# A norm's sum of squares in a two-layer transformer: one accumulator for both streams, and the last square added on VectorE

## Chip, cores and metric

The kernel runs on one core of a Trainium2 chip. The metric is the device time of one execution in microseconds (us), as a median over runs. Smaller is better. Engines are named as in the profile: PE is TensorE (matrix products), PEld its weight loads, DVE VectorE, ACT ScalarE, POOL GpSimd and SP SyncE, which here only issues transfers.

## What is computed

Two streams of 256 tokens with 1024 features each, the latent stream `x` and a context `ctx`, go through two blocks. Block 0 has a gated feed-forward network, a short convolution mixer and a second feed-forward network. Block 1 has a feed-forward network, grouped-query attention and a last feed-forward network; the context is dropped after the attention has read it. Ahead of each of the six parts both streams (in the last part only the latent one) are normalised:

```
def _rms(t, g):
    t32 = t.astype(jnp.float32)
    y = t32 * lax.rsqrt(jnp.mean(t32 * t32, axis=-1, keepdims=True) + NORM_EPS)
    return y.astype(t.dtype) * g

def _modulate(t, g, shift, scale):
    return _rms(t, g) * (1 + scale) + shift

lat = lat + 0.5 * mod[:, 0, 2] * _swiglu(_modulate(lat, norm_g[i, 0], mod[:, 0, 0], mod[:, 0, 1]), ...)
```

The change concerns `mean(t32 * t32)`, the sum of 1024 squares for each token. Everything else stays.

## The kernel before

**Layout.** Both streams lie side by side in one SBUF tile `x` of 128 partitions by 8 feature tiles by 512 tokens: `x[:, k, :]` holds features 128k to 128k+127, columns 0 to 255 are the latent stream (stream 0), columns 256 to 511 the context (stream 1). Features lie on partitions, so a sum over features is a sum over the eight tiles k, done element by element, and then a sum over 128 partitions, done on PE.

**The sum of squares.** `square_add(k, c0, c1)` (lines 254 to 268) is called once for each feature tile when that tile of `x` is final. ACT squares the tile into a buffer `sq` (line 258; one of three buffers that share the tag `gm` with other temporaries). For k = 0, DVE copies the square into the stream's accumulator `acc` (line 264); for k = 1 to 6 DVE adds it to `acc` (line 266), one instruction of 128x256 for each stream. The last square, k = 7, is not added: `accs[s, "last"]` remembers where it lies.

`rms_sum(s, parts)` (lines 270 to 285) then makes, for each of the stream's two tiles of 128 tokens, one product with a column of ones for `acc` and one for the last square, accumulated in PSUM (line 275). In float32 each such product is two records of PE. ACT takes the square root (line 280) and DVE the reciprocal (line 284). `rms_all` (line 290) spreads the 256 reciprocals over all partitions with two more products (line 293). Then `scaled` and `norm_k` or `Blocks.block` (lines 302 to 404) make the normalised tiles: a DVE instruction at line 305, ACT instructions at lines 315, 397 or 402, and DVE instructions at 316 or 398.

**Where it is called.** There are six places, and eleven streams in all:

- The first norm (lines 898 and 1055). The eight squares follow the arrival of `x`, both streams at once, while PE runs 39 products of ones on ones (`fill(WARM)`, line 1054), which stand ahead of the sums in PE's order. The order of PE, DVE, ACT and SP in this part is written out by hand (`FIRST_STEPS`).
- Four tails of `project` with `tail_norm` (line 517): after the first feed-forward network (ahead of the convolution), after the convolution, after the second feed-forward network, and after the third (ahead of attention). Here feature tiles 0 to 5 are finished for both streams at once. Tiles 6 and 7 are finished last (lines 634 to 643), first for stream 0, then for stream 1, so that stream 0's norm can start while PE still makes stream 1's products.
- One tail with `tail_early` (line 488), after attention, stream 0 only.

**What sets the order.** Outside the hand-ordered parts a planner orders each engine's instructions when the program is built: it goes through the program with a cost model and gives an engine the earliest instruction of the program that is ready. Pending pieces of a norm are put into the program by `flush` in the middle of later products. In the networks at line 784 an edge (line 792) keeps the second weight tile's products behind the last product of `rms_all` on PE. DVE, ACT and PE each work through their queue in the order so fixed. DVE's other work in these places is splitting weights into two halves (line 109, 128x1024) and a reduction of modulation weights (line 178).

Of the kernel before, what the change touches and what calls it, by code (L numbers as in the profile page):

```python
# [9 lines left out]
F32 = mybir.dt.float32  # L10
F32R = mybir.dt.float32r
BF16 = mybir.dt.bfloat16
AF = mybir.ActivationFunctionType
ALU = mybir.AluOpType
AX = mybir.AxisListType

P = 128
D = 1024
KT = D // P
S = 256  # L20
T2 = 2 * S
# [26 lines left out]
def hybrid_kernel(ctx: ExitStack, tc: tile.TileContext, a: dict, out: bass.AP):  # L48
    nc = tc.nc
# [5 lines left out]
    tp = ctx.enter_context(tc.tile_pool(name="tp", bufs=2))  # L55
# [6 lines left out]
    def nm(s):  # L62
        uid[0] += 1
        return f"{s}{uid[0]}"
# [4 lines left out]
    def psmall(s="pq"):  # L69
        return pss.tile([P, T2], F32, tag="sm", name=nm(s))  # L70
# [8 lines left out]
    x = act.tile([P, KT, T2], F32, name="x", tag="x")  # L79
    for q in range(4):  # L80
# [4 lines left out]
    ones = const.tile([P, P], F32, name="ones", tag="ones")  # L85
# [5 lines left out]
        out=const.tile([P, 1], F32, name="silu", tag="silu"), in_=eps_t, func=AF.Silu  # L91
# [132 lines left out]
    def mod_ready(l, ch):  # L224
        while not ((l, ch) in done and done[l, ch] == 8 * streams(l, ch)):
            next_unit()
        return modv[l, ch]

    def scale_of(l, j):

        m = mod_ready(l, 3 * j + 1)
        t = const.tile([P, KT, 2], F32, name=f"A{l}{j}", tag=f"A{l}{j}")
        g = normg[:, l, j, :]
        for v in range(1 if (l, j) == (1, 2) else 2):
            nc.vector.scalar_tensor_tensor(
                out=t[:, :, v], in0=m[:, :, v], scalar=1.0, in1=g, op0=ALU.add, op1=ALU.mult
            )
        return t
# [13 lines left out]
    accs = {}  # L252

    def square_add(k, c0, c1):

        n = c1 - c0
        sq = tp.tile([P, T2], F32, name=nm("sq"), tag="gm", bufs=3)
        nc.scalar.activation(out=sq[:, :n], in_=x[:, k, c0:c1], func=AF.Square)
        for s in range(2):
            if c0 <= s * S < c1:  # L260
                part = sq[:, s * S - c0 : s * S - c0 + S]
                if k == 0:
                    accs[s] = tp.tile([P, S], F32, name=nm("acc"), tag=f"acc{s}", bufs=1)
                    nc.vector.tensor_copy(accs[s], part)
                elif k < KT - 1:
                    nc.vector.tensor_tensor(out=accs[s], in0=accs[s], in1=part, op=ALU.add)
                else:
                    accs[s, "last"] = part

    def rms_sum(s, parts):  # L270

        pq = psmall("ss")
        for i in range(2):
            for n, t in enumerate(parts):
                nc.tensor.matmul(
                    pq[:, S + i : S + i + 1], t[:, i * P : i * P + P], ones[:, 0:1],
                    start=(n == 0), stop=(n == len(parts) - 1),
                )
        rs = tp.tile([P, 2], F32, name=nm("rs"), tag="rs")
        nc.scalar.activation(  # L280
            out=rs, in_=pq[:, S : S + 2], func=AF.Sqrt, scale=1.0 / D, bias=eps_t
        )
        ri = tp.tile([P, 2], F32, name=nm("ri"), tag="ri")
        nc.vector.reciprocal(ri, rs)
        return pq, ri
# [4 lines left out]
    def rms_all(pq, ri):  # L290

        for i in range(2):
            every.append(nc.tensor.matmul(
                pq[:, i * P : i * P + P], ri[:, i : i + 1].to_broadcast([P, P]), ident,
                start=True, stop=True,
            ).ins)
        return pq[:, :S]

    def rms_inv(s, parts):
        return rms_all(*rms_sum(s, parts))  # L300

    def scaled(s, k, A, ri, t=None):
        if t is None:
# [7 lines left out]
    def norm_k(s, k, h, A, B, ri, t=None):  # L311
        hh, hl = pick(h, k, s * S, s * S + S)
        t = scaled(s, k, A, ri, t)
        b = B[:, k, s : s + 1]
        nc.scalar.activation(out=hh, in_=t, func=AF.Identity, bias=b)
        nc.vector.scalar_tensor_tensor(
            out=hl, in0=t, scalar=b, in1=hh.bitcast(F32), op0=ALU.add, op1=ALU.subtract
        )
        return t
# [163 lines left out]
    def flush(n=9):  # L483
        while pending and n:
            pending.pop(0)()
            n -= 1

    def tail_early(l, j, h, z):

        box = {}  # L490

        def tail(m, c0, c1):
            if not box:
                box["A"] = scale_of(l, j)
                box["B"] = mod_ready(l, 3 * j)
                z.shift(box["B"])
            z.put(m, box["A"])
            square_add(m, c0, c1)
            if m < KT - 1:
                return  # L500

            def first():
                box["ri"] = rms_sum(0, (accs[0], accs[0, "last"]))

            def second():
                z.ri = tp.tile([P, S], F32, name=nm("ris"), tag="ris0", bufs=1)
                nc.scalar.copy(z.ri, rms_all(*box["ri"]))

            def rest(part):
                for k in range(4 * part, 4 * part + 4):  # L510
                    norm_k(0, k, h, box["A"], box["B"], z.ri)

            pending.extend((first, second, lambda: rest(0), lambda: rest(1)))

        return tail

    def tail_norm(l, j, h):

        box = {}

        def tail(m, c0, c1):
            square_add(m, c0, c1)
            if m == KT - 1:
                if not box:
                    box["A"] = scale_of(l, j)
                    box["B"] = mod_ready(l, 3 * j)
                s = c0 // S

                def inv():
                    return rms_inv(s, (accs[s], accs[s, "last"]))  # L530

                def rest(part, ri, ks=range(4)):

                    if isinstance(h, Blocks):
                        h.block(s, part, box["A"], box["B"], ri, s == 0, ks)
                    else:
                        for k in ks:
                            norm_k(s, 4 * part + k, h, box["A"], box["B"], ri)

                def both_parts():  # L540
                    ri = inv()
                    for part in range(2):
                        rest(part, ri)

                if s == 0:
                    keep = []

                    def one():
                        keep.append(inv())
                        rest(0, keep[0])  # L550

                    pending.append(one)
                    pending.append(lambda: rest(1, keep[0], range(2)))
                    pending.append(lambda: rest(1, keep[0], range(2, 4)))
                else:
                    flush()
                    pending.append(both_parts)

        return tail
# [19 lines left out]
    def ready():  # L579

        t = const.tile([P, 1], F32, name=nm("ready"), tag="ready")
        nc.scalar.activation(out=t, in_=accs[0][:, :1], func=AF.Sqrt)

    def project(ws, src, nk, gate, tail, tot, late, ev, between=()):

# [307 lines left out]
    def fill(n):  # L893

        for _ in range(n):
            nc.tensor.matmul(idle[:, :P], ones, ones, start=True, stop=True)

    for k in range(KT):
        square_add(k, 0, T2)
# [4 lines left out]
        out=sb1, in0=modb[:, 0, KT : 2 * KT], scalar1=1.0, scalar2=None, op0=ALU.add  # L904
# [147 lines left out]
    queues = [nc.tensor, nc.vector, nc.scalar, nc.sync]  # L1052
    with tc.manual_schedule(engines={e.engine for e in queues}):
        fill(WARM)
        sums = [rms_sum(s, (accs[s], accs[s, "last"])) for s in range(2)]
        for step in FIRST_STEPS.split():
            steps[step[0]](*(int(c) for c in step[1:]))
    done[0, 0] = done[0, 1] = 16
# [22 lines left out]
    for m in range(KT):  # L1081
# [4 lines left out]
        for c0, c1 in ((0, S), (S, T2)) if m == 0 else ((0, T2),):  # L1086
# [18 lines left out]
            out=d2[:, :, 1:], in0=u2[:, :, : S - 1], scalar=convk[:, 0, m : m + 1],  # L1105
            in1=d2[:, :, 1:], op0=ALU.mult, op1=ALU.add,
        )
        nc.vector.scalar_tensor_tensor(
            out=d2[:, :, : S - 1], in0=u2[:, :, 1:], scalar=convk[:, 2, m : m + 1],
            in1=d2[:, :, : S - 1], op0=ALU.mult, op1=ALU.add,  # L1110
# [70 lines left out]
    def q_proj(p):  # L1181
        wq = load_w(a["wq"][p])
        if p == 0:

            ps = [psum("pq")[:, :S] for _ in range(2)]
            order = [(i, k) for k in range(KT) for i in range(2)]
        else:
            ps = psum("pq")
            ps = [ps[:, :S], ps[:, S:], ps]
            order = [(i, k) for i in range(2) for k in range(KT)]  # L1190
        for i, k in order:
            mm3(ps[i], wq(k * 256 + i * P), pick(h, k, 0, S), k == 0, k == KT - 1)
        return ps[2:] or ps
# [60 lines left out]
    pq = [q_proj(0)]  # L1254
# [17 lines left out]
    for kv in range(KVH):  # L1272
# [7 lines left out]
        out=scq, in0=rq[:, :16], scalar1=float(P) ** -0.5, scalar2=None, op0=ALU.mult  # L1280
# [76 lines left out]
    for i in range(2):  # L1357
# [3 lines left out]
        for j in range(4):  # L1361
            c = j % 2 * T2
# [127 lines left out]
```

## Time and profile before

| | |
|---|---|
| median of 3 runs | 1559.67 us (1559.26 to 1561.86) |
| profiled execution, span from its first to its last instruction | 1558.7 us |
| profiled execution, time outside the span | not listed; the median of the runs is 0.97 us over the span |
| busy: PE, PEld, DVE, ACT, POOL | 1549.9, 1422.0, 1281.7, 782.1, 221.6 us |
| PE records of the products at line 275 | 88 |
| DVE copies at line 264, adds at line 266 | 11, 66 |
| granted TensorE clock | 1.000 |

A profile here is one execution. The page lists busy time for each engine. Waits name the engine that waited and the one that released it. The chain of work that ended last is followed backwards from the last instruction and says, at each moment, what the end hung on. A timeline row has start, length, engine, line and the tile written and read; the number behind an x says how many instructions were merged into the row. A windows row gives, for a stretch of time, busy time and instruction counts of PE, PEld, DVE, ACT and POOL, then the granted clock, the share of the DMA engines and GB/s.

### The profile page before, as it was taken

What the parts mean: (1) busy time and instruction counts of PE and PEld (TensorE: products, weight loads), DVE (VectorE), ACT (ScalarE), POOL (GpSimd) and SP (SyncE); (2) the same over time, 40 slices, a digit from 0 to 9 for tenths busy, and PEclk for the clock granted to TensorE, in tenths of its full rate; (3) what the DMA queues carried; (4) which work ended last, traced back from release to release, by engine and by line L of the source; (5) the groups of instructions that cost most, each with busy time, mean ns of one, the idle gap of its engine ahead of it and who ended that gap; (6) DMA issues with size and microseconds to landing.
All of it is one profiled execution on the core that took longest, in us unless ns stands there. A gap on an engine that the chain in (4) does not pass through costs nothing.

```text
span 1558.7 us, 26399 instructions
## 1 busy us (share of the span) xinstructions
PE 1549.9 (99%) x10296; PEld 1422.0 (91%) x10296; DVE 1281.7 (82%) x2030; ACT 782.1 (50%) x1297; POOL 221.6 (14%) x187
## 2 busy tenths in 40 slices
PE   9999999999999999999999999999999999999999
PEld 7898998999888899989999899989999898998888
DVE  5788789799987588968978888968978887888676
ACT  5642553644423366436346466436346455774553
POOL 0012213200000112032042112022042002300000
PEclk9999999999999999999999999999999999999999
DMA  9567467465555425655656635655766843276562
GB/s 371 194 173 200 109 191 193 120 194 161 191 198 178 115 62 136 205 146 130 206 144 158 200 71 136 203 149 130 235 170 170 264 156 114 93 234 219 172 197 74
DMA packets 88253, 263.53 MB, mean 169 GB/s; under 512 B 10816, under 2 KB 12608, under 8 KB 88128
## 3 DMA queue, kind: packets, MB, share of 16 engines
q1 hardware_dynamic: 69408, 230.72, 45.8%
q0 software_dynamic: 16128, 29.37, 11.3%
q10 hardware_dynamic: 2592, 1.76, 0.4%
q8 instruction: 80, 1.31, 0.3%
q14 instruction: 45, 0.37, 0.1%
HBM read 259.45 MB, written 1.05 MB: 167 GB/s over the span
## 4 chain that ended last, share of the span: by engine, by line
PE 96%; DVE 2%; ACT 1%; issue 0%; POOL 0%; DVEq 0%; ACTq 0%; POOLq 0%
PE py L137 9%; PE py L138 9%; PE py L139 9%; PE p L137 7%; PE p L139 7%; PE p L138 7%; PE q L137 5%; PE q L139 5%; PE q L138 5%; PE py L145 2%; PE pu L145 2%; PE pg L145 2%; PE py L147 1%; PE pg L147 1%; PE pu L147 1%; PE pv L138 1%
## 5 line engine op out<-in xcount | busy, mean ns | idle before, releaser
L108 ACT ACTIVATE wh<-wr 128x1024 fp32r<-128x1024 f32 (+2 forms) x446 | 394.5, 912 | 325.2 <-PE py L138 126.1
L109 DVE TENSOR_TENSOR wl<-wr,wh 128x1024 fp32r<-128x1024 f32 (+2 forms) x446 | 456.6, 1048 | 85.9 <-ACT wh L108 66.8
L178 DVE CUSTOM_DVE_ANT_0 junk<-wr,scbc,modb 128x1024 bf16<-128x1024 f32 x213 | 274.7, 1290 | 11.4 <-DMA wr<-in_modT 9.3
L137 PE MATMUL py<-gh,wh 128*128 128x512 f32 (+1 forms) x570 | 213.5, 375 | 0.0
L138 PE MATMUL py<-gl,wh 128*128 128x512 f32 (+1 forms) x570 | 213.3, 374 | 0.0
L139 PE MATMUL py<-gh,wl 128*128 128x512 f32 (+1 forms) x570 | 213.2, 374 | 0.0
L704 POOL TENSOR_SCALAR wr<-wr 128x512 f32<-128x512 f32 x56 | 101.1, 1805 | 541.7 <-DMA wr<-in_w 286.3
L567 DVE SCALAR_TENSOR_TENSOR x<-py,mod,x 128x256 f32<-128x256 f32 x213 | 94.6, 479 | 65.6 <-PE py L139 54.3
L138 PE MATMUL p<-tl,wh 128*128 128x256 f32 x448 | 126.9, 283 | 0.0
L139 PE MATMUL p<-th,wl 128*128 128x256 f32 x448 | 126.9, 283 | 0.0
L137 PE MATMUL p<-th,wh 128*128 128x256 f32 x448 | 126.9, 283 | 0.0
L139 PEld LDWEIGHTS py<-gh,wl 128*128 128x128 f32 x570 | 107.4, 188 | 19.2
L137 PEld LDWEIGHTS py<-gh,wh 128*128 128x128 f32 x570 | 107.5, 189 | 18.3
L138 PEld LDWEIGHTS py<-gl,wh 128*128 128x128 f32 x570 | 107.5, 189 | 17.9
L115 POOL DMA_DIRECT2D w4l<-in_w x56 | 53.8, 960 | 445.7 <-ACT w4l L114 431.9
L137 PE MATMUL q<-bh,wh 128*128 128x256 f32 x320 | 90.8, 284 | 0.8 <-ACT wh L108 0.8
L139 PE MATMUL q<-bh,wl 128*128 128x256 f32 x320 | 90.8, 284 | 0.0
L138 PE MATMUL q<-bl,wh 128*128 128x256 f32 x320 | 90.6, 283 | 0.0
L137 PEld LDWEIGHTS p<-th,wh 128*128 128x128 f32 x448 | 86.0, 192 | 0.3
L138 PEld LDWEIGHTS p<-tl,wh 128*128 128x128 f32 x448 | 86.0, 192 | 0.3
L139 PEld LDWEIGHTS p<-th,wl 128*128 128x128 f32 x448 | 86.1, 192 | 0.0
L764 ACT ACTIVATE sg<-sg 128x512 f32<-128x512 f32 x56 | 35.4, 632 | 90.8 <-DVE sg L763 90.6
(305 smaller groups left out, 4081.2 us busy)
## 6 DMA issues: line engine op xcount, KB each, us to landing
wr<-in_w SPq DMA_DIRECT2D x120, 512.0 KB, 4.8
wr<-in_modT SPq DMA_DIRECT2D x117, 512.0 KB, 4.9
wr<-in_w2b SPq DMA_DIRECT2D x64, 448.0 KB, 4.0
wr<-in_w2a SPq DMA_DIRECT2D x32, 512.0 KB, 4.6
wr<-in_w SPq DMA_DIRECT2D x56, 256.0 KB, 3.9
wr<-in_w POOLq DMA_DIRECT2D x56, 256.0 KB, 5.8
w4l<-in_w POOLq DMA_DIRECT2D x56, 256.0 KB, 5.9
pm<-in_mod SPq DMA_DIRECT2D x16, 512.0 KB, 10.2
```

The lines of the kernel that those rows point to most:

```text
L108: nc.scalar.activation(out=hi, in_=src, func=AF.Copy)
L109: return nc.vector.tensor_tensor(out=lo, in0=src, in1=hi.bitcast(F32), op=ALU.subtract)
L115: nc.gpsimd.dma_start(out=lo, in_=src, accum_op=ALU.add)
L137: nc.tensor.matmul(ps, wh, mh, start=first, stop=False, **kw)
L138: nc.tensor.matmul(ps, wh, ml, start=False, stop=False, **kw)
L139: nc.tensor.matmul(ps, wl, mh, start=False, stop=last, **kw)
L145: nc.tensor.matmul(ps, w[0], m[2], start=first and n == 0, stop=False)
L147: nc.tensor.matmul(ps[:, :S], w[1], m[0], start=False, stop=last and n == len(ms) - 1)
L178: nc.vector.tensor_tensor_reduce(out=junk, in0=raw, in1=scbc[:, v, :], scale=0.5 if ch in (2, 8) else 1.0, scalar=modb[:, l, col : col + 1 ...
L567: ins = nc.vector.scalar_tensor_tensor(out=x[:, m, s * S : s * S + S], in0=ps[:, o : o + S], scalar=g[:, m, s : s + 1], in1=x[:, m, s * S ...
L704: nc.gpsimd.tensor_scalar(out=r1[:, :T2], in0=r2[:, :T2], scalar1=-1.0, scalar2=None, op0=ALU.mult)
L764: nc.scalar.activation(out=self.sg, in_=self.sg, func=AF.Silu)
```

## The change

The two accumulators become one tile of 128x512 for both streams. For k = 0 ACT writes the square straight into it; the DVE copy goes. For every later k, the last included, DVE adds the square with one instruction over all the columns that the call covers: 512 where both streams are finished at once, 256 where one is. PE then makes one product for each tile of 128 tokens instead of two. `rms_sum` and `rms_inv` lose the argument `parts`, and their callers change accordingly; `ready()` reads column 0 of the common accumulator.

```diff
     def square_add(k, c0, c1):
-        n = c1 - c0
+        if k == 0:
+            accs["t"] = tp.tile([P, T2], F32, name=nm("acc"), tag="acc", bufs=1)
+            nc.scalar.activation(out=accs["t"][:, c0:c1], in_=x[:, k, c0:c1], func=AF.Square)
+            return
         sq = tp.tile([P, T2], F32, name=nm("sq"), tag="gm", bufs=3)
-        nc.scalar.activation(out=sq[:, :n], in_=x[:, k, c0:c1], func=AF.Square)
-        for s in range(2):
-            if c0 <= s * S < c1:
-                part = sq[:, s * S - c0 : s * S - c0 + S]
-                if k == 0:
-                    accs[s] = tp.tile([P, S], F32, name=nm("acc"), tag=f"acc{s}", bufs=1)
-                    nc.vector.tensor_copy(accs[s], part)
-                elif k < KT - 1:
-                    nc.vector.tensor_tensor(out=accs[s], in0=accs[s], in1=part, op=ALU.add)
-                else:
-                    accs[s, "last"] = part
-
-    def rms_sum(s, parts):
+        nc.scalar.activation(out=sq[:, : c1 - c0], in_=x[:, k, c0:c1], func=AF.Square)
+        t = accs["t"][:, c0:c1]
+        nc.vector.tensor_tensor(out=t, in0=t, in1=sq[:, : c1 - c0], op=ALU.add)
+
+    def rms_sum(s):
         pq = psmall("ss")
         for i in range(2):
-            for n, t in enumerate(parts):
-                nc.tensor.matmul(
-                    pq[:, S + i : S + i + 1], t[:, i * P : i * P + P], ones[:, 0:1],
-                    start=(n == 0), stop=(n == len(parts) - 1),
-                )
+            c = s * S + i * P
+            nc.tensor.matmul(
+                pq[:, S + i : S + i + 1], accs["t"][:, c : c + P], ones[:, 0:1],
+                start=True, stop=True,
+            )
...
     def ready():
         t = const.tile([P, 1], F32, name=nm("ready"), tag="ready")
-        nc.scalar.activation(out=t, in_=accs[0][:, :1], func=AF.Sqrt)
+        nc.scalar.activation(out=t, in_=accs["t"][:, :1], func=AF.Sqrt)
```

More of the change, by code (lines that the diff above doesn't have):

```diff
@@ L297, in rms_all, with rms_inv @@
         return pq[:, :S]
-    def rms_inv(s, parts):
-        return rms_all(*rms_sum(s, parts))
+    def rms_inv(s):
+        return rms_all(*rms_sum(s))
     def scaled(s, k, A, ri, t=None):
@@ L502, in first @@
             def first():
-                box["ri"] = rms_sum(0, (accs[0], accs[0, "last"]))
+                box["ri"] = rms_sum(0)
             def second():
@@ L529, in inv @@
                 def inv():
-                    return rms_inv(s, (accs[s], accs[s, "last"]))
+                    return rms_inv(s)
                 def rest(part, ri, ks=range(4)):
@@ L1054, in hybrid_kernel @@
         fill(WARM)
-        sums = [rms_sum(s, (accs[s], accs[s, "last"])) for s in range(2)]
+        sums = [rms_sum(s) for s in range(2)]
         for step in FIRST_STEPS.split():
```

## The prediction, made before the result was known

> **What bounds the kernel now.** I read the page's first part, then the chain that ended last.
>
> ```profile
> span 1558.7 us, 26399 instructions
> ...
> PE 1549.9 (99%) x10296; PEld 1422.0 (91%) x10296; DVE 1281.7 (82%) x2030; ACT 782.1 (50%) x1297; POOL 221.6 (14%) x187
> ...
> PE 96%; DVE 2%; ACT 1%; issue 0%; POOL 0%; DVEq 0%; ACTq 0%; POOLq 0%
> ```
>
> PE is busy for all but 8.8 us, and 96% of the chain lies on it. So PE work that goes away shortens the run wherever PE does not then stand and wait for another engine. An average cannot say where it would; I asked for windows around the norms (columns: length, busy PE, PEld, DVE, ACT, POOL, clock, DMA share, GB/s).
>
> ```profile
> 380.00:392.00 12.00, 11.98 (x99) 11.59 (x97) 12.00 (x28) 5.60 (x13) 0.00 (x0) 1.00 0.31 102
> 555.00:565.00 10.00, 10.00 (x86) 10.00 (x86) 8.74 (x20) 8.34 (x21) 0.00 (x0) 1.00 0.02 8
> 565.00:590.00 25.00, 24.55 (x206) 24.33 (x204) 22.49 (x30) 17.80 (x27) 2.37 (x2) 1.00 0.17 42
> 903.00:915.00 12.00, 11.55 (x93) 10.97 (x92) 9.95 (x22) 9.43 (x22) 0.43 (x1) 1.00 0.32 87
> 1256.00:1266.00 10.00, 10.00 (x86) 10.00 (x86) 9.69 (x23) 7.30 (x14) 0.00 (x0) 1.00 0.13 32
> 1362.00:1378.00 16.00, 16.00 (x137) 16.00 (x136) 11.51 (x19) 12.19 (x23) 0.00 (x0) 1.00 0.61 194
> ```
>
> These are the tails ahead of the convolution (380), of the second network (555, 565), of the third network (903), of attention (1256), and the latent-only tail (1362). PE is full nearly everywhere. But DVE is full too ahead of the convolution (12.00 of 12) and nearly so ahead of attention (9.69 of 10), and ahead of the third network PE already waits 0.45 us. There PE is fast enough to catch up with DVE, and freed PE time may only become waiting.
>
> **PE: what goes.** The products are at line 275; the chain shows what they take between their neighbours.
>
> ```profile
> L275 PE MATMUL ss<-ones,acc x44: 164/250/251, 12.7 to 1372.5; 128*128 128x1 f32 x44
> L275 PE MATMUL ss<-ones,sq x44: 164/250/271, 12.8 to 1372.8; 128*128 128x1 f32 x44
> 12.85 1.68 PE ss L275 x16
> 553.58 0.79 PE ss L275 x8
> 1253.43 0.84 PE ss L275 x8
> ```
>
> A record lasts 250 ns, but 16 take 1.68 us and 8 about 0.80: they overlap, one each 0.10 us. The 44 records that read `sq` go. That is 8 in the first norm (half of 1.68, **0.84 us**) and 4 in each of nine later streams (half of 0.79, **0.40 us**, in all 3.6). More than 0.84 + 3.6 = **4.4 us** cannot come from PE.
>
> **DVE: what goes, comes and is merged.** Rows of one copy, one add, a 512-wide add of another line, and of two 256-wide adds in a row:
>
> ```profile
> L264 DVE COPY acc<-sq x11: 282/286/295, 6.4 to 1354.0; 128x256 f32<-128x256 f32 x11
> L266 DVE TENSOR_TENSOR acc<-acc,sq x66: 415/420/427, 6.8 to 1369.5; 128x256 f32<-128x256 f32 x66
> L763 DVE TENSOR_TENSOR sg<-q,sg 128x512 f32<-128x512 f32 x56 | 38.6, 689 | 4.5 <-PE q L139 3.6
> 356.22 0.49 DVE L264 COPY acc<-sq 128x256 f32<-128x256 f32 x2
> 357.05 0.76 DVE L266 TENSOR_TENSOR acc<-acc,sq 128x256 f32<-128x256 f32 x2
> ```
>
> Two adds of 0.42 take 0.76, so the next one starts 0.34 after the first; a 512-wide add of 0.69 then takes some 0.61 of the queue. Before: 11 copies by 0.245 and 66 adds by 0.34, 25.1 us. After: 27 adds of 512 (7 in the first norm, 5 in each of four tails) by 0.61 and 23 of 256 (2 streams by 2 in four tails, 7 in the latent-only tail) by 0.34, 24.3 us. DVE as a whole gains 0.8 us: nothing. The place matters: the gain lies early in a tail, in the copies and merged adds, and the new add of k = 7 lies at its end, one per stream.
>
> The Trainium skill ("VectorE: DVE Perf Modes", section "The DRAIN you can't avoid") says that the next VectorE operation does not start until the pipe is empty. By that, two adds would take 0.84 and a merge would give DVE 0.15 instead of 0.07; five merges ahead of the convolution, where DVE is full, would give 0.4 us more, and my sum would come to 1556.8. The pair above, 0.76 and not 0.84, speaks against it.
>
> The copy that goes costs no wait: ACT's write is of the same size as before (the `sq` buffer and the accumulator are both SBUF). The common tile could tie the streams to each other, if stream 1's add had to wait for PE's reading of stream 0's columns. I cost this at nothing, as those products stand in the program ahead of stream 1's seventh square; if not, the price is one such product group, 0.4 us in each of four tails.
>
> **The last add on the path.** Before, the last square went straight from ACT to PE. Now it goes through DVE's queue. Ahead of the convolution:
>
> ```profile
> 374.50 1.28 DVE L178 CUSTOM_DVE_ANT_0 junk<-wr,scbc,modb 128x1024 bf16<-128x1024 f32 x1
> 374.68 0.42 ACT L258 ACTIVATE sq<-x 128x256 f32<-128x256 f32 x1 [1.51 <-DVE x L567]
> 374.81 0.28 PE L275 MATMUL ss<-ones,acc 128*128 128x1 f32 x2
> 375.87 0.28 PE L275 MATMUL ss<-ones,sq 128*128 128x1 f32 x2
> 376.64 0.26 ACT L280 ACTIVATE rs<-ss,eps_t 128x2 f32<-128x2 f32 x1 [1.54 <-PE ss L275]
> ```
>
> The square is ready at 375.10. If DVE is free the add ends some 0.5 us later (0.42 and a hand-over of 0.05), and the products, one half of before, take 0.4 less: the inverse comes 0.1 us later than now. If DVE has just begun a long operation, the add waits up to 1.28 more; here until 375.78, and the inverse comes at about the same time as today, because PE had put its products late anyway. Behind the waiting add on DVE stand the `t` instructions of line 305 and weight splits of line 109, for which ACT and then PE wait. So between 0.1 and 1.4 us later for each stream, with cover: PE has other products to make meanwhile.
>
> **Place by place.** First norm:
>
> ```profile
> 1.05 11.81 PE idle L896 x78
> 10.27 1.15 ACT L258 ACTIVATE sq<-x 128x512 f32<-128x512 f32 x2 [1.31 <-DVE acc L266]
> 11.44 1.28 ACT L280 ACT_TABLE_LOAD   x1
> 20.30 0.50 PE L999 MATMUL pg<-hh,wh 128*128 128x512 f32 x1 [0.23 <-ACT hh L972]
> ```
>
> The last square ends at 11.42; the new 512-wide add by 12.2. The warming products end at 12.86 and the table load at 12.72, so the add is hidden with 0.6 us to spare; without that cover it would cost 0.7. PE's chain goes on with the modulation products at once, so all **0.84** is gained.
>
> Ahead of the convolution DVE is the limit at the end of the norm: PE arrives 0.8 earlier and waits for DVE. Between -0.8 and +0.5 (one long operation ahead of an add, less the cover); I take **-0.1**, near the DVE-bound end. Ahead of the second network DVE has spare time (8.74 of 10) and PE is full up to the sums of stream 1: -0.8 to 0, I take **-0.6**. Ahead of the third:
>
> ```profile
> 912.69 0.40 ACT L258 ACTIVATE sq<-x 128x256 f32<-128x256 f32 x1
> 913.20 1.22 DVE L109 TENSOR_TENSOR wl<-wr,wh 128x1024 fp32r<-128x1024 f32 x1
> 914.33 1.23 DVE L398 SCALAR_TENSOR_TENSOR bl<-t,mod,bh 128x256 fp32r<-128x256 f32 x2
> 914.87 0.39 PE L138 MATMUL pg<-bl,wh 128*128 128x256 f32 x1 [0.35 <-DVE bl L398]
> ```
>
> PE waits at 914.87 for DVE. The new add comes in front of that, 0.34 of DVE's queue, and the PE time freed just before is spent waiting: -0.4 to +1.2, I take **+0.3**. Ahead of attention PE never waits, but DVE is nearly full: -0.8 to +0.5, I take **-0.6**. The latent-only tail has DVE at 11.5 of 16 and its sums come long after the last square: **-0.4**.
>
> Sum: -0.84 - 0.1 - 0.6 + 0.3 - 0.6 - 0.4 = **-2.2 us**. Against the span of 1558.7 that is 1556.5; what lies outside the span (0.97 us to the median) stays, so the median of 1559.67 becomes **1557.4**, 0.14% less.
>
> **Rivals.** *All freed PE time is kept.* For it: PE full in every window; the planner fills gaps with other products. Against it: DVE at 12.00 of 12. Time: 1559.67 - 4.4 = 1555.2.
>
> *DVE swallows it.* Only the first and the latent-only tail gain, 0.84 + 0.4: 1558.4.
>
> *The last add queues behind DVE's long operations, and the run gets slower.* Place: the two-stream tails, where stream 1's sums release the second weight tile on PE by the fence of line 792. Today the reciprocal leaves little in hand there:
>
> ```profile
> 565.03 0.17 DVE L284 RECIPROCAL ri<-rs 128x2 f32<-128x2 f32 x1 [0.48 <-ACT rs L280]
> 565.83 0.60 PE L293 MATMUL ss<-ident,ri 128*128 128x128 f32 x4
> ```
>
> From the end of `ri` to its product are 0.6 us; PE comes there 0.8 earlier after the change. Price: up to 1.28 + 0.42 + 0.06 - 0.40 = 1.4 us for each of the four stream-1 sums, and as much again where stream 0's chain is bare, in four tails 5.4; less the 1.24 of the other two places, +4.2, or 1563.9. It decides once an add starts later than 0.6 us after its square. For it: rows of 1.28 and 1.22 stand at just these spots. Against it: the planner knows these lengths and today puts its short instructions between them.
>
> That the change does not do what it says is no case: PE's second product, the copies and the wide adds are explicit instructions.
>
> **Chances.** The sum above 0.38, all kept 0.17, swallowed 0.14, slower 0.31. About 0.2% (3.1 us) is what a measurement of this kernel can tell from no change. The sum's own range, the ends of the places taken together in part, is -3.6 to -0.8, 1556.1 to 1558.9; 0.11 of it lies below 1556.55. Faster: 0.17 + 0.11 = 0.28. Slower: 0.28 of the 0.31. Within: 0.27 + 0.14 + 0.03 = 0.44. The range 1555.0 to 1563.0 leaves out the best few hundredths of "all kept" and some 0.13 of "slower".
>
> **What would show it.** Line 275 with 44 records, at 0.1 us each; no row at line 264; PE idle longer ahead of the convolution and at 915, unchanged elsewhere; the first main product, now at 20.30, near 19.5. I am wrong upward if PE waits in front of line 293 or of line 398's readers by more than 0.5 us in several tails, and wrong downward if DVE's order closes up so that PE does not wait more than today.

## The result, and the profile after

The changed kernel takes 1556.69 us (median of 13 runs, 1556.15 to 1558.97); the kernel before, run beside it, 1560.23 (13 runs, 1559.26 to 1562.36). The ratio is 0.9980, 95% interval 0.9973 to 0.9987: 3.5 us less. The profiled execution took 1558.75 us with a span of 1557.0; in every run that lists both, the time is some 1.8 us above the span.

The first part of the page and its chain, after:

```profile
span 1557.0 us, 26280 instructions
...
PE 1545.5 (99%) x10252; PEld 1416.9 (91%) x10252; DVE 1284.5 (82%) x2003; ACT 781.9 (50%) x1297; POOL 221.8 (14%) x187
...
PE 96%; DVE 2%; ACT 1%; DMA 1%; issue 0%; POOL 0%; ACTq 0%; DVEq 0%; POOLq 0%
```

PE lost 44 records and is busy for 4.4 us less, the bound that the prediction gave. That the two agree to the tenth is partly chance: in this execution the warming was 1.4 us shorter, and a slow clock at the start made PE's work some 1.7 longer (both below). The rows of the products (line 270) and of the adds (line 263), each with its count, shortest, median and longest duration in ns:

```profile
L270 PE MATMUL ss<-ones,acc x44: 164/250/272, 13.0 to 1371.0; 128*128 128x1 f32 x44
...
L263 DVE TENSOR_TENSOR acc<-acc,sq x50: 416/684/693, 6.6 to 1369.3; 128x512 f32<-128x512 f32 x27, 128x256 f32<-128x256 f32 x23
```

So the instructions are the forecast ones. To see where the time went, one instruction serves as a milestone: the one that finishes a piece of `x` (line 567 before, 562 after). There are 213 in both kernels, in the same order. Two of them, at the end of the second network and at the end of attention, before:

```profile
881.35 0.88 DVE L567 SCALAR_TENSOR_TENSOR x<-py,mod,x 128x256 f32<-128x256 f32 x2 [0.90 <-PE py L139]
...
1351.72 0.87 DVE L567 SCALAR_TENSOR_TENSOR x<-py,mod,x 128x256 f32<-128x256 f32 x2
```

and after:

```profile
883.35 0.88 DVE L562 SCALAR_TENSOR_TENSOR x<-py,mod,x 128x256 f32<-128x256 f32 x2 [0.90 <-PE py L139]
...
1350.41 0.87 DVE L562 SCALAR_TENSOR_TENSOR x<-py,mod,x 128x256 f32<-128x256 f32 x2
```

At 881 the changed kernel is 2.00 late, at 1352 it is 1.31 early. Between two milestones this difference moves in steps, one at each norm, and is flat elsewhere. The step at each of the six places, in us, each from the difference before it to the difference after it:

| place | forecast | changed kernel | product twice | last add only | joined only | four places |
|---|---|---|---|---|---|---|
| first norm | -0.84 | +0.99 | +1.17 | -0.88 | -1.14 | -1.18 |
| convolution | -0.1 | +0.33 | +1.22 | +0.79 | -0.15 | -0.02 |
| 2nd network | -0.6 | +0.68 | +1.12 | +0.68 | -0.01 | +0.01 |
| 3rd network | +0.3 | -0.79 | -0.35 | -0.81 | 0.00 | -0.81 |
| attention | -0.6 | -2.52 | -1.59 | -2.50 | -0.01 | -2.49 |
| latent-only tail | -0.4 | -0.45 | -0.05 | -0.47 | -0.02 | -0.47 |

The columns on the right are experiments, below. The first row says little: it compares single executions, and the unchanged beginning already differs by some 1.2 us from one to the next, mostly by the length of the warming (last section); in the other rows kernels with the same code at a place agree within 0.2, mostly within 0.02. The total is near the forecast; hardly one of its terms is. Four readings show what happened.

**First norm.** PE and DVE:

```profile
1.05 10.42 PE L891 MATMUL idle<-ones 128*128 128x128 f32 x78 [1.05 <-DVE eps_t L88]
11.49 1.49 DVE L263 TENSOR_TENSOR acc<-acc,sq 128x512 f32<-128x512 f32 x2 [0.97 <-ACT sq L261]
13.04 1.05 PE L270 MATMUL ss<-ones,acc 128*128 128x1 f32 x8 [1.56 <-DVE acc L263]
21.29 0.50 PE L994 MATMUL pg<-hh,wh 128*128 128x512 f32 x1 [0.23 <-ACT hh L967]
```

The warming ended at 11.47 and not at 12.86, the adds at 12.98 and not at 12.2. PE stood 1.56 us, and then ran at half clock from 14.36 to 17.77 (windows in the last section). The eight products take 1.05 where the sixteen took 1.84 by the same rows (12.69 to 14.53), 0.8 less as forecast, but the first main product comes at 21.29 instead of 20.30. This execution has a mean clock of 0.999. So have two more of the 13 runs, with spans of 1556.9 and 1557.2; the other ten have 1.000 and spans of 1554.3 to 1555.8.

**Ahead of the convolution**, stream 0's last square and what follows it:

```profile
375.32 1.28 DVE L178 CUSTOM_DVE_ANT_0 junk<-wr,scbc,modb 128x1024 bf16<-128x1024 f32 x1
375.50 0.42 ACT L261 ACTIVATE sq<-x 128x256 f32<-128x256 f32 x1 [1.67 <-DVE x L562]
...
376.52 0.42 DVE L263 TENSOR_TENSOR acc<-acc,sq 128x256 f32<-128x256 f32 x1
...
377.32 1.06 ACT L108 ACTIVATE wh<-wr 128x1024 fp32r<-128x1024 f32 x1 [1.40 <-PE py L138]
...
378.29 0.25 ACT L275 ACTIVATE rs<-ss,eps_t 128x2 f32<-128x2 f32 x1
...
380.71 1.06 ACT L108 ACTIVATE wh<-wr 128x1024 fp32r<-128x1024 f32 x1 [1.66 <-PE py L138]
381.68 1.29 ACT L310 ACTIVATE hh<-t,mod 128x256 fp32r<-128x256 f32 x3
...
382.22 0.39 PE L137 MATMUL pv<-hh,wh 128*128 128x256 f32 x1 [1.43 <-ACT hh L310]
```

The square is ready at 375.92, and the add waits 0.60 for a reduction of 1.28. That much the prediction had. It had not that one delay begets the next: the root now stands behind a weight split of 1.06 in ACT's queue and comes 2.37 after the square (before: 375.10 to 376.64, 1.54); and `hh`, whose `t` starts at 379.88, stands behind another weight split, for which ACT first waits 1.66 on PE to free a buffer. From the square to `hh` are 5.76 us, before it was 3.67 (375.10 to 378.77). PE pays 1.43 for it.

**Ahead of the second network**, stream 1:

```profile
563.94 0.43 DVE L263 TENSOR_TENSOR acc<-acc,sq 128x256 f32<-128x256 f32 x1
...
566.35 0.24 ACT L275 ACTIVATE rs<-ss,eps_t 128x2 f32<-128x2 f32 x1
...
566.48 1.23 DVE L109 TENSOR_TENSOR wl<-wr,wh 128x1024 fp32r<-128x1024 f32 x1
...
567.62 0.16 DVE L279 RECIPROCAL ri<-rs 128x2 f32<-128x2 f32 x1
567.83 0.52 PEld L288 LDWEIGHTS ss<-ident,ri 128*128 128x128 f32 x4 [0.90 <-DVE ri L279]
```

The root is ready at 566.59, DVE has begun a split at 566.48, and the reciprocal comes 1.03 us late. Behind it stands the fence of the second weight tile: PE waits 0.7 us.

**Ahead of attention** time was won, more than the products could give. Line 1300 (1295 after) takes the maximum of the first scores, line 1302 (1297) turns it into the bias `nb` of the exponential. Before:

```profile
1307.84 0.69 DVE L1300 TENSOR_REDUCE mx<-psc 128x1 f32<-128x512 f32 x1 [1.08 <-PE psc L139]
...
1311.36 0.21 DVE L1302 TENSOR_SCALAR nb<-mx,scq 128x1 f32<-128x1 f32 x1
```

After:

```profile
1306.30 1.28 DVE L109 TENSOR_TENSOR wl<-wr,wh 128x512 fp32r<-128x512 f32 x2
1308.88 0.69 DVE L1295 TENSOR_REDUCE mx<-psc 128x1 f32<-128x512 f32 x1 [1.29 <-PE psc L139]
...
1310.12 0.21 DVE L1297 TENSOR_SCALAR nb<-mx,scq 128x1 f32<-128x1 f32 x1
```

Before, two weight splits and two rotations stood in DVE's queue between the maximum and its bias: 3.52 us from start to start. After, the two splits stand ahead of the maximum and the two rotations behind the bias, which comes after 1.24. DVE waits for the scores ahead of the maximum in both kernels, 1.08 and 1.29. The same can be read off the waits of PE (engine, tile and line, releaser, us in total, times, longest), before and then after:

```profile
PE pt L1337 <- ACT e L1313: 0.8, 1, 0.8
...
PE psc L137 <- DVE ptl L109: 0.6, 1, 0.6
...
PE psc L137 <- ACT e L1313: 0.2, 1, 0.2
PE pt L1337 <- POOL pn L1324: 0.2, 1, 0.2
```

```profile
PE ss L270 <- DVE acc L263: 1.6, 1, 1.6
PE pv L137 <- ACT hh L310: 1.4, 1, 1.4
...
PE ss L288 <- DVE ri L279: 0.7, 1, 0.7
...
PE pg L137 <- ACT bh L392: 0.5, 1, 0.5
...
PE pt L1332 <- POOL pn L1319: 0.2, 1, 0.2
PE psc L137 <- DVE ptl L109: 0.2, 1, 0.2
```

Attention's waits fell from 1.8 to 0.4 us; of the four new waits above these in the second list the first three are those of the first norm, the convolution and the second network, and the 0.5 for `bh` lies ahead of the third. No run moves the two splits alone; that they are what is won is read from these rows, and from their place in the experiments below.

### The profile page after: what moved, and what is told of

Its sections match the earlier page's. It is cut to its first block, busy times and chain, and to the rows that moved or that the text cites. A ratio compares the mean times of both kernels' runs of the same rounds, so it can differ in the third digit from the quotient of the medians.

```text
span 1557.0 us, 26280 instructions
## 1 busy us (share of the span) xinstructions
PE 1545.5 (99%) x10252; PEld 1416.9 (91%) x10252; DVE 1284.5 (82%) x2003; ACT 781.9 (50%) x1297; POOL 221.8 (14%) x187
## 3 DMA queue, kind: packets, MB, share of 16 engines
q8 instruction: 80, 1.31, 0.3%
HBM read 259.45 MB, written 1.05 MB: 167 GB/s over the span
## 4 chain that ended last, share of the span: by engine, by line
PE 96%; DVE 2%; ACT 1%; DMA 1%; issue 0%; POOL 0%; ACTq 0%; DVEq 0%; POOLq 0%
PE py L138 9%; PE py L137 9%; PE py L139 9%; PE p L137 7%; PE p L139 7%; PE p L138 7%; PE q L137 5%; PE q L139 5%; PE q L138 5%; PE py L145 2%; PE pu L145 2%; PE pg L145 2%; PE py L147 1%; PE pg L147 1%; PE pu L147 1%; PE pv L137 1%
## 6 DMA issues: line engine op xcount, KB each, us to landing
pm<-in_mod SPq DMA_DIRECT2D x16, 512.0 KB, 10.2
```

## Experiments

The theory after the result: the PE time of the products is kept almost everywhere, full DVE or not, and beside it the last add shifts the order of the queues, at a loss ahead of the convolution and the second network and a gain ahead of attention. The rival: the gain comes from DVE, which is relieved of copies and split adds. Each kernel keeps the code of before at the places not named (a switch by place moves their line numbers by some 3 to 28). Times are medians; the kernel before had 1560.24 us (33 runs) beside the first four and 1560.14 (30 runs) beside the last four.

### The first norm alone

```diff
-        sums = [rms_sum(s, (accs[s], accs[s, "last"])) for s in range(2)]
+        sums = [rms_sum(s) for s in range(2)]
```

`square_add` is the changed one for this norm, and that of before for the others.

> The first norm alone is changed (common accumulator, last square added on VectorE, one product per token tile); the five tails stay as before. Theory A (the freed products are the gain where PE bounds): the first main product, at 20.30 us before, comes 0.84 us earlier and everything behind it by as much; time 0.8 us less than before, ratio 0.9995. Rival B (the last add ends behind the warming products, PE stands idle, its clock drops): the first main product comes up to 1.0 us later, as in the profile of the changed kernel (21.29 us), with a granted clock near 0.8 between 12 and 20 us. Both may be seen, in different executions, if the arrival of the input varies.

Measured: 1559.64 us (1559.45 to 1561.13), ratio 0.9996, interval 0.9988 to 1.0005. By the medians the first norm is worth 0.6, which the interval does not tell from nothing. In its profile PE waited 0.36 us ahead of the products, and the clock was 1.00.

### The later norms alone

```diff
-                box["ri"] = rms_sum(0, (accs[0], accs[0, "last"]))
+                box["ri"] = rms_sum(0)
-                    return rms_inv(s, (accs[s], accs[s, "last"]))
+                    return rms_inv(s)
```

Their `square_add` is the changed one, the first norm's that of before.

> The five tails are changed, the first norm stays as before. From the profile of the changed kernel, place by place: ahead of the convolution +0.3, ahead of the second network +0.7, ahead of the third -0.8, attention -2.5, latent-only tail -0.45; sum -2.75 us, ratio 0.9982. Theory A with freed PE time alone would give at most 3.6 us, spread as 0.8 for each two-stream tail.

Measured: 1557.33 us (1556.48 to 1558.14), ratio 0.9982, interval 0.9973 to 0.9991. That is -2.9; with the -0.6 of the first norm -3.5, the whole of the gain.

### The norm ahead of attention alone

The same diff, at that one tail.

> Only the norm ahead of attention is changed. Theory A (freed PE products): -0.8 us, all of it won before 1270 us. Rival C (the planner's new order of VectorE in the projections brings the second key tile's norm earlier, so that the start of the softmax no longer waits): -2.3 to -2.5 us, of which over 1.5 between 1300 and 1323 us, and PE's waits at the first transposes shrink from about 2 us to 0.5.

Measured: 1557.68 us (1556.99 to 1558.56), ratio 0.9984, interval 0.9975 to 0.9992: -2.6, and the step at attention is -2.52, with the other steps within 0.1 of nothing. One of six places brings most of the gain, and the products that go there take only 0.8 us: the rest needs another cause. Maximum to bias takes 1.24 here too (1307.74 to 1308.98).

### Every product made twice

```diff
+                for _ in range(2):
                     nc.tensor.matmul(
                         pq[:, S + i : S + i + 1], t[:, i * P : i * P + P], ones[:, 0:1],
                         start=True, stop=True,
                     )
```

> The changed kernel, with each product of the column sums made twice into the same place, so that PE has as many of these products as before while VectorE's work and order are those of the changed kernel. Theory A (freed products are the gain): nearly all of it is lost again, 1559.7 to 1560.5 us, ratio to before about 1.000. Rival C (order of the other engines): 0.84 is lost at the start, 0.4 in the latent-only tail, 0.8 ahead of the third network, little where PE waits for VectorE; about 1558.7 us, ratio 0.999, and attention keeps its 2 us.

Measured: 1561.84 us (1560.51 to 1562.82), ratio 1.0009, interval 1.0000 to 1.0018. The time is above both expectations. PE has as many records as before, and DVE's order is that of the changed kernel, instruction for instruction, so the column "product twice" of the table is the order alone: +1.22, +1.12, -0.35, -1.59, -0.05, in sum +0.35. The difference to the changed kernel's column is the products alone: -0.89, -0.44, -0.44, -0.93, -0.40, in sum -3.1 of the 3.6 that they took. The order ahead of attention is the new one:

```profile
1311.72 0.69 DVE L1323 TENSOR_REDUCE mx<-psc 128x1 f32<-128x512 f32 x1 [1.29 <-PE psc L142]
1312.96 0.21 DVE L1325 TENSOR_SCALAR nb<-mx,scq 128x1 f32<-128x1 f32 x1
```

Maximum to bias takes 1.24. In this kernel PE waited 0.80 us for the last add of the first norm, and the clock fell too:

```profile
14.00:16.00 2.00, 2.00 (x20) 0.88 (x19) 0.17 (x1) 0.30 (x2) 0.00 (x0) 0.63 1.06 428
16.00:18.00 2.00, 2.00 (x12) 1.78 (x16) 0.48 (x1) 0.75 (x3) 0.00 (x0) 0.51 0.99 393
```

Six of its 11 runs show a clock of 0.999, which lifts its median above what was expected. The order's +0.35 alone would give 1560.6; the median of the five runs with a clock of 1.000 is 1560.80.

### The last add alone

```diff
                 if k == 0:
                     accs[s] = tp.tile([P, S], F32, name=nm("acc"), tag=f"acc{s}", bufs=1)
                     nc.vector.tensor_copy(accs[s], part)
-                elif k < KT - 1:
+                else:
                     nc.vector.tensor_tensor(out=accs[s], in0=accs[s], in1=part, op=ALU.add)
-                else:
-                    accs[s, "last"] = part
```

and one product for each token tile.

> Part of the change alone, everywhere: the two accumulators and their two first copies stay as before, but the last square is added on VectorE and each token tile has one column-sum product. Nothing of the computation is left out. Theory of the products (what PE no longer does is kept nearly whole, with the order of the queues on top): the same 44 products go as in the changed kernel, so -0.6 at the first norm and about -3.1 in the other norms, and the order effects of the last add (convolution +1.2, 2nd network +1.1) stay; the better order ahead of the attention may or may not appear, since the copies are still in the plan: 1556.5 to 1558.5 us against 1560.2. Rival, that the gain comes from the common accumulator (first squares without copies): 1560 or more, since VectorE gets work here and loses none.

Measured: 1557.28 us (1556.64 to 1557.82), ratio 0.9981, interval 0.9972 to 0.9990. That is 2.9 of the 3.5 us, with more work on DVE than before (1286.1 against 1281.7 us busy, 11 instructions more), and it has the new order ahead of attention:

```profile
1307.46 0.69 DVE L1322 TENSOR_REDUCE mx<-psc 128x1 f32<-128x512 f32 x1 [1.29 <-PE psc L142]
...
1308.70 0.21 DVE L1324 TENSOR_SCALAR nb<-mx,scq 128x1 f32<-128x1 f32 x1
```

Only ahead of the convolution is its step 0.46 worse than the changed kernel's (+0.79 against +0.33): there, with the last add in the queue, the copies and split adds on DVE, or the order that comes with them, do cost.

### The common accumulator alone

```diff
+        if k == 0:
+            accs["t"] = tp.tile([P, T2], F32, name=nm("acc"), tag="acc", bufs=1)
+            nc.scalar.activation(out=accs["t"][:, c0:c1], in_=x[:, k, c0:c1], func=AF.Square)
+            return
+        if k < KT - 1:
+            nc.vector.tensor_tensor(out=t, in0=t, in1=sq[:, : c1 - c0], op=ALU.add)
```

The last square stays in `sq`, and a second product of each token tile sums it, as before.

> The other part alone, everywhere: one accumulator of both streams, the first square written into it directly, additions over both streams at once; the last square still goes into its own tile and is summed by a second product of each token tile, as before. Nothing of the computation is left out. Theory of the products: PE does as much as before, so no gain from it; the last add is not on VectorE, so the losses of the convolution and the 2nd network (+1.2, +1.1) are gone too; what is left is the order that the planner finds, at most -1.6 if the two weight splits go ahead of the first maximum of the attention: 1558.5 to 1560.5 us. Rival, that relieving VectorE is what counts: 1557.5 or less, since VectorE has copies and split additions taken off and nothing added.

Measured: 1560.13 us (1558.97 to 1561.19), ratio 0.9999, interval 0.9990 to 1.0008. Its page:

```profile
PE 1548.6 (99%) x10296; PEld 1420.4 (91%) x10296; DVE 1277.5 (82%) x1993; ACT 782.2 (50%) x1297; POOL 223.5 (14%) x187
```

DVE has 37 instructions fewer and is busy for 4.2 us less (1281.7 before), and the time does not move. (Busy sums are no finer than some 2 us: the changed kernel and the one with doubled products have the same DVE instructions, and 1284.5 and 1282.4.) All its steps behind the first norm are within 0.15 of nothing. Ahead of attention the order is the old one:

```profile
1306.53 0.69 DVE L1322 TENSOR_REDUCE mx<-psc 128x1 f32<-128x512 f32 x1 [1.86 <-PE psc L142]
...
1310.06 0.21 DVE L1324 TENSOR_SCALAR nb<-mx,scq 128x1 f32<-128x1 f32 x1
```

3.53 from maximum to bias. The rival falls on both sides: relief of DVE alone brings nothing, and the last add with one product for each tile, with DVE busier, four fifths of the gain.

### More warming

```diff
-WARM = 39
+WARM = 43
```

> The changed kernel with 43 instead of 39 warming products ahead of the column-sum products of the first norm, nothing else. Nothing of the computation is left out. Theory that a gap between the end of the warming and the last add lets the granted clock fall: four more products take 4 x 0.27 = 1.07 us at the pace of the profile of the changed kernel, the gap of 1.56 us there falls to about 0.5, the clock stays at 1.00 in the first 20 us in all runs, and no run has the longer span of about 1557; the median stays at 1556.3 to 1557.3, because in the executions without a drop the added warming costs up to 0.5. Rival, that the low clock at the start has another cause (it comes at a fixed time, or with the modulation's first product): some of the runs still show a clock under 1.00 and a span of 1557 and more, and all become later by up to 1 us.

Measured: 1557.40 us (1556.45 to 1558.23), ratio 0.9981, interval 0.9972 to 0.9989. All of its 11 runs have a clock of 1.000. Its first norm:

```profile
1.05 12.40 PE L918 MATMUL idle<-ones 128*128 128x128 f32 x86 [1.05 <-DVE eps_t L91]
13.28 0.95 PE L297 MATMUL ss<-ones,acc 128*128 128x1 f32 x8
19.96 0.50 PE L1021 MATMUL pg<-hh,wh 128*128 128x512 f32 x1 [0.23 <-ACT hh L994]
```

No wait and no fall of the clock, which agrees with the theory of the gap but does not prove it: the changed kernel shows a lower clock in only 3 of 13 runs, so that none in 11 could be chance. But the warming now ends 0.9 after the last add (12.53), which delays every execution. By these numbers it swaps a loss of some 2 us in a few runs for one of some 0.8 in all, and the median ends 0.1 above the top of what was expected.

### Four places

```diff
+NEW = {(0, 0), (1, 0), (1, 1), (1, 2)}
-            return (accs[s], accs[s, "last"])
+            return (accs[s],) if j in NEW else (accs[s], accs[s, "last"])
```

`j` is the layer and the norm in it, and `square_add` follows the same switch: the change everywhere except ahead of the convolution, (0, 1), and ahead of the second network, (0, 2).

> The change at four of its six places: first norm, ahead of the 3rd network, ahead of the attention, and latent-only; the convolution's tail and the norm ahead of the 2nd network as before. Nothing of the computation is left out. If the offsets of the places add up: first norm -0.6, 3rd network -0.8, attention -2.5, latent-only -0.45, in sum -4.35: 1555.9 us. Rival, that the planner's order at one place depends on what other places do, so that a place's effect can't be taken over by itself: anywhere from 1556.5 to 1559.5, and the maximum of the attention or the tail of the convolution is where the offsets differ from those of the changed kernel.

Measured: 1555.91 us (1555.42 to 1557.38, 8 runs), ratio 0.9974, interval 0.9963 to 0.9984. The steps add up: each place behind the first norm has the step that it has in the changed kernel, or nothing where the code is that of before. This version is faster than the kernel before by 4.2 us and, each against its own runs of before, 0.7 below the changed kernel, a difference that lies within the two intervals. The profiled execution has a span of 1553.8; in its first norm PE waits 0.68 us, and the clock stays at 1.00:

```profile
12.38 1.05 PE L297 MATMUL ss<-ones,acc 128*128 128x1 f32 x8 [0.68 <-DVE acc L273]
```

## Why the prediction was right in sum and wrong in its places

**Right.** The time lies in the range, 0.7 below the number given; the median of the kernel before had moved up by 0.6, so the gain is 3.5 where 2.2 was forecast. The range says little, since 1555.0 to 1563.0 also holds no change at all. The counts, the 0.1 us for a product, the common tile at no cost (the only engine that the adds waited for was ACT), and the latent-only term (-0.4 forecast, -0.45 found) held.

**Wrong: "freed PE time may only become waiting".** This step set the convolution to -0.1, on the ground that DVE was busy for 12.00 of 12 us there, and it made the third network a loss, on the ground that PE already waits for DVE. The doubled products show that PE's part is worth 0.89 ahead of the convolution, the whole of the 0.8 and a little more, and 0.44 ahead of the second and the third network. There the step is right by half. Stream 0's part is kept. Of stream 1's nothing is left: in the changed kernel PE's next instruction starts 0.72 and 0.80 after the first of its last group of column sums, with doubled products 0.81 and 0.81, because PE waits for `bl`, `ri` or `bh` behind them.

The common accumulator alone shows DVE's side: 4.2 us less on DVE bring nothing. In the full window of 12 us DVE spent 9.0 on `t` and `hl` (lines 305 and 316), which PE's products need, and 2.4 on weight splits, and PE still stood for no more than 0.02. A full window says that an engine has no gap, not that anybody waits for it. PE's own waits, 0.45 us in the third network's window and none ahead of the convolution and attention, would have been the better row to go by. Ahead of the second network even they would have missed: PE does not wait at that norm before, and its waits there came with the new order. So the rival "all freed PE time is kept" had more of the mechanism than the sum: 3.5 is nearer to its 4.4 than to 2.2, and behind the first norm 3.1 of 3.6 was kept. What it lacked is the order.

**Wrong in place: the rival of the last add.** Its mechanism, a wait behind a long DVE operation, is in the trace in two of four tails (0.60 of the add behind a reduction, 1.03 of the reciprocal behind a split), and the order there is worth +1.22 and +1.12. The forecast named the fence of the second weight tile for it, and PE does wait 0.7 there. But the forecast counted one delay where there was a chain: the add, then a weight split of ACT ahead of the root, then another ahead of `hh`. And its condition, an add that starts more than 0.6 after its square, is not what decides: ahead of the convolution it was 0.60, and ahead of the second network the add started at once (square ready at 563.90, add at 563.94) and the time was lost later, the last 1.03 of it at the reciprocal.

**Missed: attention.** -0.6 forecast, -2.5 found. Of it -0.93 are the products (0.8 forecast as the most) and -1.59 the new order, which no term and no rival held. The prediction looked at the queues as they stood and asked what an added instruction would do to its neighbours there; the planner made a new order. That it comes with the last add, and not with the common accumulator, is shown by the two halves of the change; why the planner's reckoning then puts the splits ahead of the maximum was not tried.

**Wrong: "hidden with 0.6 us to spare"** at the first norm. The length of the warming was taken from one execution. It was 11.81 there, and between 10.42 and 11.93 in eight others with the same 39 products, by when the clock came up (last section), and the 512-wide adds ended between 12.30 and 12.98, not at 12.2. In all four profiles with these adds and 39 products the cover is missing: PE waits 0.36, 0.68, 0.80 and 1.56. With a short warming the first norm gains nothing in the traces: the first main product comes at 19.16 and 19.15 with eight products (the first norm alone, four places), and at 19.09 and 19.16 with sixteen (the later norms alone, the common accumulator alone). In the two profiles with the longest gaps the clock fell besides. By the medians 0.6 of the 0.84 is left, within the noise.

Two smaller slips: in the sum for two adds that do not overlap, 0.4 us more takes 1557.4 to 1557.0 and not to 1556.8; and the 0.97 us "outside the span" sets the median of three runs against the span of one execution, where the runs have some 1.8; it does not touch the gain.

That the sum came near is luck: three errors of sign (convolution, second and third network) and one of size (attention) cancelled in part. The five later places were put at -1.4 and brought -2.75, which is -3.1 for the products and +0.35 for the order on balance.

## What to carry to other kernels

Where PE is the bound, price freed PE time in full unless PE is seen to wait right behind it, whatever the busy share of the engine that feeds it. (This is read off after the fact, from four tails of one kernel, and the wait can be one that the change itself brings.) An instruction added to another engine's queue is to be followed through each queue that its result passes, since a shift of half a microsecond can set it behind a long operation at every one of them. Where a planner lays out the order, single places can move by more than the edit itself, so try the change place by place and keep it where it pays.

## What the runs showed of the hardware

The clock at the start was not expected, in two ways. The first sets the length of the warming. The records of the warming follow each other by 0.213 us, and later by 0.112. The pace changes at 7.0 us in the profile of before and at 4.1 in that of the changed kernel. Their rows from 4.2 on, eleven records in one and twenty in the other:

```profile
4.19 2.56 PE L896 MATMUL idle<-ones 128*128 128x128 f32 x11
4.27 2.40 PE L891 MATMUL idle<-ones 128*128 128x128 f32 x20
```

2.9 us more at about half the pace are some 1.4 us, the difference between 11.81 and 10.42. (The clock column of the windows reads 1.00 there from the start, so it does not show this.) The second is a fall of the clock later. Windows in the changed kernel, with the granted clock behind POOL:

```profile
14.00:14.50 0.50, 0.50 (x9) 0.29 (x13) 0.22 (x2) 0.26 (x1) 0.00 (x0) 0.86 0.98 401
14.50:17.00 2.50, 2.50 (x18) 1.61 (x11) 0.09 (x1) 0.50 (x2) 0.00 (x0) 0.50 1.03 419
...
17.50:18.00 0.50, 0.50 (x9) 0.29 (x12) 0.26 (x1) 0.28 (x1) 0.00 (x0) 0.73 1.02 418
```

The clock is half, from about 14.36 (a mean of 0.86 over half a microsecond is 0.14 us at half rate) to about 17.77: 3.4 us, which cost 1.7. It starts 1.3 us after PE had its first product again. In the kernel with doubled products it lasts from about 14.5 to 18.0. In both the fall comes 10.2 us after the clock came up (at 4.1 and 4.3), three times the 3.4. A gap of 0.80 us came with a fall there, one of 0.68 did not in the kernel of four places; but the doubled kernel also has sixteen products of one column behind its gap, and the other eight.

The Trainium skill ("TensorE: Matmul & The Clock Gate", section "What's actually happening") has a gate at half rate that looks at free-running windows of about 3.4 us. Half rate and length agree with this trace, and a window that runs free of the program would explain why the clock comes up at another time in each execution and why only some are hit. That section asks for an idle window, and PE here was idle for 0.8 to 1.56 us of it, and for another 1 to 2 us made products of one column. What share of a window counts as idle was not measured, and that the gap is the cause is not shown: the kernel before is hit too, in 10 of the 63 runs beside the experiments, and the common accumulator alone in 3 of 11, and the profiles of both show no gap.
